# Attention of a two-layer decoder: the negative maximum and the first exponential of a row of scores are issued ahead of the filling work, evacuations queue behind them in one tile, and the reciprocals are turned one block later

## The chip, the cores and the metric

The kernel runs on one core of a Trainium2 chip. A core has a matrix engine (TensorE, PE in the profile), a vector engine (VectorE, DVE), an activation engine (ScalarE, ACT), GpSimd (POOL) and a queue engine (SyncE, SP). Each engine works through its own list of instructions in the order in which they stand in the program, and waits on semaphores for the others. The metric is the device time of one execution in microseconds (us).

## The reference

A model of two layers on 2048 tokens of width 1024: a Mamba-2 mixer, then causal attention with 16 heads over keys and values made once from a compressed latent, then an output projection and a last norm, all in float32. The part that the change touches is the attention:

```python
s = einsum('bqhd,bkhd->bhqk', q_nope, k_nope) + einsum('bqhr,bkr->bhqk', q_rope, k_rope)
s = s.astype(float32) * scale
p = softmax(where(mask, s, -inf), axis=-1)
o = einsum('bhqk,bkhd->bqhd', p, v)
```

## The kernel before

The program has three stages after each other: the Mamba layer with all projections, the attention (`heads`, from L1181), and the output projection (`back`). In the attention, the work on PE is issued in the order in which the Python code records it (a manual schedule for PE alone). For DVE, ACT, POOL and SP a list scheduler puts the recorded instructions in an order at build time; on the chip that order is fixed, and an instruction that waits holds back all that stand behind it on its engine.

Each of the 16 heads has four blocks of 512 queries (qb 0 to 3). A block has four query tiles of 128 queries (j 0 to 3). The scores of a query tile against all keys up to the diagonal are computed in banks of up to 512 keys: one bank for qb 0, two for qb 1, three for qb 2, four for qb 3. Below, **S qb.j.n** is the n-th bank of scores of query tile j. The steps for a query tile, in `scores` (L1197):

- S: three matmuls (L88 to L90, fp16 in high and low halves) into a PSUM bank with the tag `mm`; there are four such banks. In the last bank a fourth matmul adds the causal mask (L1220).
- DVE takes the maximum of each bank (`mx`, L1221) and, after the last one, the negative maximum over all of them (`nm`, L1225).
- ACT takes exp(s + nm) of each bank into `Pr` (L1233) and sums the row beside it. Only then is the `mm` bank free for a later S. In the profile this exponential is an ACTIVATE followed by a short ACTIVATION_READ_ACCUMULATOR, which carries the release. These are put on a list `late` and recorded one by one before the score banks of the next query tile.
- DVE adds the sums of the banks to one number per row (`sum`, L1237).

The exponentials become an output in two more steps, for each block of queries and each of its 4qb+4 tiles of 128 keys (kb):

- **T qb.kb** (`turn`, L1243): up to four transposes on PE (L1248) into a bank with the tag `tr`, of which there are four too; ACT evacuates the high half (`PTs`, L119), DVE the low half (L120).
- **V qb.kb** (`values`, L1254): two matmuls (L1258, L1259) that add the product with the values to the output bank of the block, also a `tr` bank. After the last kb, ACT copies that bank out (`Os`, L1265), and two DMAs add its halves in memory.

What fills PE while a query tile's maximum and exponentials run is the T and V work of a block that lies up to 20 banks of scores back. The table CREDIT (L44) says, for each qb, j and bank, which T and V units are recorded after that bank. After the last block of a head, DVE takes the reciprocals of the 16 sums per row (`ri`, L1274 and L1275), PE turns them (L1277) into a `tr` bank, ACT copies them (`rT`, L1279), and they go to memory.

Of the kernel before, what the change touches and what calls it, by code (L numbers as in the profile page):

```python
# [21 lines left out]
P = 128  # L22
# [22 lines left out]
    (("VT",), ("TV",), ("VT",), ("TV",)),  # L45
    (("", "VTVT"), ("", "TTVV"), ("", "TTVV"), ("", "TTVV")),
    (("TT", "", "VVTV"), ("TV", "", "VTTV"), ("TV", "", "TTVV"), ("TTV", "", "TVV")),
    (("T", "", "", "VVTTVTV"), ("T", "V", "", "VTTVTV"), ("T", "V", "V", "TVTTV"), ("TV", "V", "", "TVTVT")),
)
MAGIC = 12582912.0  # L50
PSCALE = 32768.0
# [20 lines left out]
class Net:  # L72
# [1108 lines left out]
    def heads(self, sp):  # L1181
# [15 lines left out]
        def scores(h, qb, st):  # L1197

            if h + 1 < NH:
                if qb == 2:  # L1200
                    self.load_k(h + 1, 0, NB)
                    self.load_v(h + 1)
                self.load_q(h + 1, qb)
            Q, K = quer.pop((h, qb)), keys[h]
            late = []
            for j in range(4):
                qs = slice(j * P, (j + 1) * P)
                parts = cuts(qb * TB + (j + 1) * P)
                nb = len(parts)
                mx = self.t(sp, "mx", [P, 4], bufs=4)  # L1210
                banks = []
                for n, (c0, w) in enumerate(parts):
                    if late:
                        late.pop(0)()
                    begun.append(0)
                    s = self.t(self.pp, "tr" if len(begun) <= 18 and len(begun) % 2 == 1 else "mm", [P, TB], bufs=4)
                    ks = slice(c0, c0 + w)
                    self.mm3(s[:, :w], Q[:, 0, qs], Q[:, 1, qs], K[:, 0, ks], K[:, 1, ks], True, n < nb - 1)
                    if n == nb - 1:
                        nc.tensor.matmul(s[:, w - P:w], self.idb, self.mk, start=False, stop=True)  # L1220
                    v.tensor_reduce(mx[:, n:n + 1], s[:, :w], AX.X, ALU.max)  # L1221
                    banks.append((s, w))
                    yield CREDIT[qb][j][n]
                nm = self.t(sp, "nm", [P, 1], bufs=4)
                v.tensor_reduce(nm, mx[:, :nb], AX.X, ALU.max, negate=True)  # L1225
                p = {}
                sm = self.t(sp, "sm", [P, 4], bufs=4)
                st["P"].append(p)

                def exp(n, j=j, nb=nb, parts=parts, banks=banks, nm=nm, p=p, sm=sm):  # L1230
                    s, w = banks[n]
                    x = self.t(sp, "Pr", [P, TB], bufs=NP)
                    nc.scalar.activation(x[:, :w], s[:, :w], AF.Exp, bias=nm, accum_out=sm[:, n:n + 1])  # L1233
                    for c in range(0, w, P):
                        p[(parts[n][0] + c) // P] = x[:, c:c + P]
                    if n == nb - 1:
                        v.tensor_reduce(sums[h][:, 4 * qb + j:4 * qb + j + 1], sm[:, :nb], AX.X, ALU.add)  # L1237

                late += [lambda n=n, f=exp: f(n) for n in range(nb)]
            for f in late:  # L1240
                f()

        def turn(h, qb, kb, st):  # L1243

            jj = max(kb - 4 * qb, 0)
            pt = self.t(self.pp, "tr", [P, TB], bufs=4)
            for j in range(jj, 4):
                nc.tensor.transpose(pt[:, j * P:(j + 1) * P], st["P"][j][kb], self.ident)  # L1248
# [14 lines left out]
        def finish(h, qb, st):  # L1263
# [8 lines left out]
            if qb == NB - 1:  # L1272
                ri = self.t(sp, "ri", [P, 16], bufs=2)
                v.reciprocal(ri, sums[h])  # L1274
                v.tensor_scalar(ri, ri, 0.5, None, ALU.mult)  # L1275
                ps = self.t(self.pp, "tr", [P, TB], bufs=4)
                nc.tensor.transpose(ps[:16, 0:P], ri, self.ident)  # L1277
# [7 lines left out]
        def ahead():  # L1285
            for n, (h, qb) in enumerate(jobs):
                if qb == 0:
                    sums[h] = self.t(sp, "sum", [P, 16], bufs=3)
                yield from scores(h, qb, states[n])

        units = [(h, qb, kb, states[n]) for n, (h, qb) in enumerate(jobs) for kb in range(4 * qb + 4)]
# [11 lines left out]
        step = 0  # L1303
# [206 lines left out]
```

## Time and profile before

| what | value |
|---|---|
| time, median of 3 runs | 3100.96 us (3096.12 to 3102.59) |
| time of the profiled execution | 3099.32 us |
| its span, first to last instruction | 3097.2 us, so 2.1 us lie around it |
| busy in the span | PE 97%, DVE 75%, ACT 63%, POOL 20% |
| attention, from the first bank of scores to the last transposes | 2007.8 to 2906.5 us |
| one head of the attention in the middle | 55.63 us |

A row of the timeline gives the start in us from the start of the span, the length, the engine, the line, the operation, output and inputs by the program's tile names, how many instructions are merged in it, and, in brackets, how long the engine sat idle just before and what ended that. A matmul row is longer than the time until the next matmul can start: matmuls are pipelined, and rows of 0.38 us start every 0.22 us. So a wait of PE is the distance between two starts less 0.22 us (for 512 columns; 0.16 for 384, 0.11 for 256, 0.06 for 128), which is up to 0.16 us more than the idle time in brackets.

### The profile page before, as it was taken

To read this page: it belongs to the slowest core of one execution; us is meant where nothing else is said; L and a number is where in the kernel's file an instruction comes from. 1 tells how busy PE (TensorE), PEld (TensorE's weight loads), DVE (VectorE), ACT (ScalarE), POOL (GpSimd) and SP (SyncE) were. 2 spreads that over 40 slices of the span, in tenths; PEclk is the share of its full clock that TensorE was granted. 3 is DMA by queue.
4 is the path that set the end of the run, shared out by engine and by line. 5 is a ranking of instruction groups with operands and counts; after the bars stand their busy time and mean duration, and the time that the engine had idled before them with its cause. 6 is when DMAs were issued, how large, how long until landed. Compare 5 with 4: busy or idle time off the path is not lost.

```text
span 3097.2 us, 51355 instructions
## 1 busy us (share of the span) xinstructions
PE 2994.5 (97%) x17758; PEld 1759.2 (57%) x17758; DVE 2330.1 (75%) x5306; ACT 1936.4 (63%) x4920; POOL 615.3 (20%) x842
## 2 busy tenths in 40 slices
PE   7899999999999999999999999999999999999998
PEld 3466655555455554545555555456666666665777
DVE  7789887777777687797755453488888888888576
ACT  8777566665667656565534333388888888888422
POOL 0211122211222112222111212322122222222100
PEclk9999999999999999999999999999999999999999
DMA  8675436445454466364466555622223222232485
GB/s 298 221 235 181 151 106 220 129 158 163 153 191 162 131 207 222 121 199 145 145 214 197 194 173 170 197 49 60 55 56 67 54 58 57 54 88 75 130 261 158
DMA packets 205065, 457.11 MB, mean 148 GB/s; under 512 B 28114, under 2 KB 57554, under 8 KB 203364
## 3 DMA queue, kind: packets, MB, share of 16 engines
q1 hardware_dynamic: 176948, 375.94, 37.9%
q0 software_dynamic: 27856, 77.89, 9.8%
q8 instruction: 140, 2.29, 0.3%
q14 instruction: 121, 0.99, 0.1%
HBM read 340.99 MB, written 112.73 MB: 146 GB/s over the span
## 4 chain that ended last, share of the span: by engine, by line
PE 40%; DVE 5%; ACT 4%; issue 3%; DMA 2%; POOL 0%; SPq 0%; ACTq 0%; POOLq 0%; DVEq 0%
PE mm L88 7%; PE mm L90 6%; PE mm L89 6%; PE tr L1248 6%; PE tr L1259 3%; PE tr L1258 3%; PE tr L88 3%; PE tr L90 3%; PE tr L89 3%; ACT Pr L1233 2%; DVE PTs L120 1%; DMA os<-ri_d 1%; ACT PTs L119 1%; DVE mx L1221 1%; PE mm L1220 0%
## 5 line engine op out<-in xcount | busy, mean ns | idle before, releaser
L120 DVE SCALAR_TENSOR_TENSOR PTs<-tr,PTs 128x512 f16<-128x512 f32 (+3 forms) x640 | 374.2, 606 | 76.8 <-ACT PTs L119 69.7
L1233 ACT ACTIVATE Pr<-mm,nm 128x512 f32<-128x512 f32 (+2 forms) x631 | 394.2, 635 | 49.4 <-DVE nm L1225 44.9
L1221 DVE TENSOR_REDUCE mx<-mm 128x1 f32<-128x512 f32 (+2 forms) x631 | 373.1, 604 | 31.1 <-PE mm L90 28.3
L119 ACT ACTIVATE PTs<-tr 128x512 f16<-128x512 f32 (+3 forms) x640 | 329.4, 544 | 97.9 <-PE tr L1248 95.9
L1248 PE MATMUL tr<-pack,Pr 128*128 128x128 f32 x2176 | 317.5, 273 | 1.8 <-ACT Os L1265 1.4
L88 PE MATMUL mm<-xT,wsp 128*128 128x512 f16 x800 | 305.7, 382 | 7.9 <-ACT wsp L119 4.9
L89 PE MATMUL mm<-xT,wsp 128*128 128x512 f16 x800 | 304.6, 381 | 0.0
L90 PE MATMUL mm<-xT,wsp 128*128 128x512 f16 x800 | 303.6, 380 | 0.0
L1248 PEld LDWEIGHTS tr<-pack,Pr 128*128 128x128 f32 x2176 | 253.2, 141 | 68.9 <-ACT Os L1265 2.2
L88 PE MATMUL mm<-K,xT 96*128 96x512 f16 (+2 forms) x639 | 222.4, 348 | 27.5 <-ACT Pr L1233 24.0
L88 PE MATMUL mm<-wsp,xT 128*128 128x512 f16 (+1 forms) x640 | 232.0, 363 | 4.3 <-ACT craw L610 4.1
L89 PE MATMUL mm<-wsp,xT 128*128 128x512 f16 (+1 forms) x640 | 232.3, 363 | 3.0 <-DVE wsp L120 3.0
L89 PEld LDWEIGHTS <-xT 128*128 128x128 f16 (+1 forms) x1408 | 138.0, 98 | 168.1 <-issue 69.6
L616 DVE SCALAR_TENSOR_TENSOR cacc<-craw,pack,cacc 128x512 f32<-128x512 f32 x288 | 219.3, 790 | 18.0 <-ACT cacc L614 17.2
L90 PE MATMUL mm<-wsp,xT 128*128 128x512 f16 (+1 forms) x640 | 232.5, 364 | 0.0
L90 PE MATMUL mm<-K,xT 96*128 96x512 f16 (+2 forms) x639 | 221.8, 347 | 0.0
L89 PE MATMUL mm<-K,xT 96*128 96x512 f16 (+2 forms) x639 | 221.2, 346 | 0.0
L1258 PE MATMUL tr<-PTs,xT 128*128 128x512 f16 (+3 forms) x640 | 221.0, 347 | 0.1
L1259 PE MATMUL tr<-PTs,xT 128*128 128x512 f16 (+3 forms) x640 | 219.1, 347 | 0.0
L90 PEld LDWEIGHTS <-xT 128*128 128x128 f16 (+1 forms) x1408 | 136.9, 97 | 133.1 <-issue 5.7
L88 PEld LDWEIGHTS <-xT 128*128 128x128 f16 (+1 forms) x1408 | 137.7, 98 | 120.1 <-issue 8.5
L88 PE MATMUL mm<-wsp,yT 128*128 128x512 f16 (+1 forms) x512 | 197.4, 385 | 0.9 <-DVE sz L640 0.5
(456 smaller groups left out, 6795.8 us busy)
## 6 DMA issues: line engine op xcount, KB each, us to landing
wsp<-wi_d SPq DMA_DIRECT2D x96, 512.0 KB, 3.6
big<-cumT SPq DMA_DIRECT2D x64, 512.0 KB, 4.8
wraw<-in_ssm_w_out_dram SPq DMA_DIRECT2D x96, 256.0 KB, 3.6
wi_d<-wsp SPq DMA_DIRECT2D x32, 512.0 KB, 3.8
wsp<-wo_d SPq DMA_DIRECT2D x32, 512.0 KB, 3.5
wsp<-wu_d SPq DMA_DIRECT2D x28, 512.0 KB, 3.8
hx<-in_ssm_w_in_dram SPq DMA_DIRECT2D x48, 256.0 KB, 4.8
wraw<-in_ssm_w_in_dram SPq DMA_DIRECT2D x48, 256.0 KB, 4.4
```

The source lines that it names most:

```text
L88: mm(out, l_hi, r_hi, start=start, stop=False)
L89: mm(out, l_hi, r_lo, start=False, stop=False)
L90: mm(out, l_lo, r_hi, start=False, stop=stop)
L119: self.nc.scalar.activation(hi, src, AF.Copy, scale=scale)
L120: self.nc.vector.scalar_tensor_tensor(lo, src, scale, hi, ALU.mult, ALU.subtract)
L616: nc.vector.scalar_tensor_tensor(acc, raw[:, k:k + TB], wk[k], acc, ALU.mult, ALU.add)
L1221: v.tensor_reduce(mx[:, n:n + 1], s[:, :w], AX.X, ALU.max)
L1233: nc.scalar.activation(x[:, :w], s[:, :w], AF.Exp, bias=nm, accum_out=sm[:, n:n + 1])
L1248: nc.tensor.transpose(pt[:, j * P:(j + 1) * P], st["P"][j][kb], self.ident)
L1258: nc.tensor.matmul(st["O"][:, c], vals[h][:, kb, :], u[:, 0], start=kb == 0, stop=False)
L1259: nc.tensor.matmul(st["O"][:, c], vals[h][:, kb, :], u[:, 1], start=False, stop=kb == nk - 1)
```

## The change

Five things, all in the attention:

1. The negative maximum `nm` is recorded directly after the last maximum of a query tile, before the T and V units that CREDIT puts behind that bank; it used to be recorded after them. With one bank (qb 0) the maximum itself is taken with a minus sign, and `nm` falls away.
2. Where a query tile has three or four banks (qb 2 and 3), its first exponential is recorded directly after `nm` too.
3. In the first query tile of qb 3 (j 0, four banks) a list `pins` makes the evacuations of the T units that follow it stand behind that `nm` on DVE and behind that first exponential on ACT.
4. The sums of a block's four query tiles go to one tile, and DVE adds them up in one instruction per block (none for qb 0, where ACT writes the sum itself), not one per query tile.
5. The reciprocals are computed where they were, but turned by PE and copied by ACT after the output of the next head's first block, and CREDIT is changed for the first two query tiles of qb 3: the T unit after the first bank of j 0 goes to the end of j 0, and one T and one V unit from the end of j 0 go to the first bank of j 1.

```diff
-    (("T", "", "", "VVTTVTV"), ("T", "V", "", "VTTVTV"), ("T", "V", "V", "TVTTV"), ("TV", "V", "", "TVTVT")),
+    (("", "", "", "TVVTTV"), ("TVT", "V", "", "VTTVTV"), ("T", "V", "V", "TVTTV"), ("TV", "V", "", "TVTVT")),
...
-            late = []
+            late, total = [], sums[h][:, 4 * qb:4 * qb + 4]
+            sm = self.t(sp, "sm", [P, 4, 4], bufs=2) if qb else total.unsqueeze(2)
...
-                    v.tensor_reduce(mx[:, n:n + 1], s[:, :w], AX.X, ALU.max)
                     banks.append((s, w))
+                    if nb == 1:
+                        v.tensor_reduce(nm, s[:, :w], AX.X, ALU.max, negate=True)
+                    else:
+                        v.tensor_reduce(mx[:, n:n + 1], s[:, :w], AX.X, ALU.max)
+                    if n == nb - 1:
+                        if nb > 1:
+                            self.last_max = v.tensor_reduce(nm, mx[:, :nb], AX.X, ALU.max, negate=True)
+
+                        def exp(n, j=j, nb=nb, parts=parts, banks=banks, nm=nm, p=p):
+                            s, w = banks[n]
+                            x = self.t(sp, "Pr", [P, TB], bufs=NP)
+                            self.last_exp = nc.scalar.activation(x[:, :w], s[:, :w], AF.Exp, bias=nm,
+                                                                 accum_out=sm[:, j, n:n + 1])
+                            for c in range(0, w, P):
+                                p[(parts[n][0] + c) // P] = x[:, c:c + P]
+                            if j == 3 and n == nb - 1 and nb > 1:
+                                v.tensor_reduce(total, sm[:, :, :nb], AX.X, ALU.add)
+
+                        late += [lambda n=n, f=exp: f(n) for n in range(nb)]
+                        if nb > 2:
+                            late.pop(0)()
+                        if nb > 3 and j == 0:
+                            pins[:] = [self.last_max, self.last_exp]
                     yield CREDIT[qb][j][n]
-                nm = self.t(sp, "nm", [P, 1], bufs=4)
-                v.tensor_reduce(nm, mx[:, :nb], AX.X, ALU.max, negate=True)
...
-            self.pair16(u[:, 0, c], u[:, 1, c], pt[:, c], PSCALE)
+            with ExitStack() as order:
+                for pin in pins:
+                    order.enter_context(self.tc.issue_after(pin.ins))
+                self.pair16(u[:, 0, c], u[:, 1, c], pt[:, c], PSCALE)
...
                 v.tensor_scalar(ri, ri, 0.5, None, ALU.mult)
+                inverse.append((h, ri))
+            if inverse and (qb == 0 or h == NH - 1):
+                h, ri = inverse.pop()
                 ps = self.t(self.pp, "tr", [P, TB], bufs=4)
                 nc.tensor.transpose(ps[:16, 0:P], ri, self.ident)
...
         for credit in ahead():
             step += 1
             if step > LAG:
                 for what in credit:
                     work(what)
+            pins.clear()
```

The diff tells what is recorded; where the scheduler then puts it is another matter. Three places, all in the eighth head (heads 2 to 14 have the same order).

**First place: DVE, end of qb 2.** Before, from the last two maxima of S 2.3 on (`mx_5665`, from the banks `mm_5677` and `mm_5679`): the sum of the tile before, the negative maximum (`nm_5683`), the low half of T 1.0 (`PTs_5681`), then the first maxima of qb 3.

```order
L1221 TENSOR_REDUCE mx_5665_27502<-mm_5677_27537 128x1
L1221 TENSOR_REDUCE mx_5665_27502<-mm_5679_27545 128x1
L1237 TENSOR_REDUCE sum_5543_27076<-sm_5664_27501 128x1
L1225 TENSOR_REDUCE nm_5683_27564<-mx_5665_27502 128x1
L120 SCALAR_TENSOR_TENSOR PTs_5681_27556<-tr_5680_27551,PTs_5681_27556 128x512
L1221 TENSOR_REDUCE mx_5689_27578<-mm_5690_27579 128x1
```

After the change, the same stretch (`mx_5566` is the maxima, `nm_5567` the negative maximum, `PTs_5581` the low half of T 1.0, `nm_5588` the negative maximum of S 3.0, `PTs_5595` that of T 1.1):

```order
L1228 TENSOR_REDUCE mx_5566_27272<-mm_5577_27303 128x1
L1228 TENSOR_REDUCE mx_5566_27272<-mm_5578_27308 128x1
L120 SCALAR_TENSOR_TENSOR PTs_5581_27322<-tr_5580_27317,PTs_5581_27322 128x512
L1231 TENSOR_REDUCE nm_5567_27273<-mx_5566_27272 128x1
L1228 TENSOR_REDUCE mx_5587_27340<-mm_5589_27342 128x1
L1228 TENSOR_REDUCE mx_5587_27340<-mm_5590_27347 128x1
L1241 TENSOR_REDUCE sum_5452_26866<-sm_5525_27117 128x4
L1228 TENSOR_REDUCE mx_5587_27340<-mm_5591_27352 128x1
L1228 TENSOR_REDUCE mx_5587_27340<-mm_5592_27357 128x1
L1231 TENSOR_REDUCE nm_5588_27341<-mx_5587_27340 128x1
L120 SCALAR_TENSOR_TENSOR PTs_5595_27371<-tr_5594_27366,PTs_5595_27371 128x512
```

Here the negative maximum of S 2.3 has moved behind the low half of T 1.0, while that of S 3.0 stands directly behind its maxima, ahead of T 1.1.

**Second place: ACT, start of qb 3.** Before, from the last exponential of S 2.3 (`Pr_5687`): T 1.1, the copy of the output of qb 0 (`Os_5696`), T 1.2 to T 1.4, then the four exponentials of S 3.0 (their first is `Pr_5707`).

```order
L1233 ACTIVATE Pr_5687_27571,sm_5684_27566<-mm_5679_27545,nm_5683_27564 128x512
L119 ACTIVATE PTs_5692_27589<-tr_5691_27584 128x512
L1265 ACTIVATE Os_5696_27612<-tr_5682_27559 128x512
L119 ACTIVATE PTs_5698_27621<-tr_5697_27616 128x512
L119 ACTIVATE PTs_5700_27629<-tr_5699_27624 128x512
L119 ACTIVATE PTs_5703_27640<-tr_5702_27635 128x512
L1233 ACTIVATE Pr_5707_27649,sm_5705_27647<-mm_5690_27579,nm_5704_27645 128x512
L1233 ACTIVATE Pr_5711_27663,sm_5705_27647<-mm_5693_27592,nm_5704_27645 128x512
```

After the change (`Pr_5584` is the last exponential of S 2.3, `Pr_5593` and `Pr_5606` the first two of S 3.0, `PTs_5595` T 1.1, `PTs_5600` T 1.2, `rT_5598` the copy of the turned reciprocals of the head before):

```order
L1236 ACTIVATE Pr_5584_27332,sm_5525_27117<-mm_5578_27308,nm_5567_27273 128x512
L1236 ACTIVATE Pr_5593_27364,sm_5586_27339<-mm_5589_27342,nm_5588_27341 128x512
L119 ACTIVATE PTs_5595_27371<-tr_5594_27366 128x512
L1277 ACTIVATE Os_5596_27378<-tr_5582_27325 128x512
L1294 ACTIVATE rT_5598_27384<-tr_5597_27382 16x128
L119 ACTIVATE PTs_5600_27392<-tr_5599_27387 128x512
L1236 ACTIVATE Pr_5606_27408,sm_5586_27339<-mm_5590_27347,nm_5588_27341 128x512
```

The first exponential of S 3.0 has moved ahead of T 1.1 and of the copy of qb 0's output; the other three now alternate with evacuations. On PE, T 1.3 now takes the `tr` bank that this copy frees (before, T 1.4 did), and V 1.0 opens its output bank in the one that the copy `rT` frees.

**Third place: DVE, qb 0 of the next head.** Before, from the negative maximum of S 0.1 on (`nm_5556`): the last sum of the head before, the reciprocal, the low half of T 2.9 of the head before (`PTs_5548`), a sum, the maximum of S 0.2 (`mx_5558`).

```order
L1225 TENSOR_REDUCE nm_5556_27118<-mx_5551_27100 128x1
L1237 TENSOR_REDUCE sum_5317_26274<-sm_5538_27066 128x1
L1274 RECIPROCAL ri_5673_27527<-sum_5317_26274 128x16
L120 SCALAR_TENSOR_TENSOR PTs_5548_27094<-tr_5547_27090,PTs_5548_27094 128x384
L1237 TENSOR_REDUCE sum_5543_27076<-sm_5550_27099 128x1
L1221 TENSOR_REDUCE mx_5558_27121<-mm_5560_27125 128x1
```

After the change (`nm_5460` and `nm_5466` are the negative maxima of S 0.1 and S 0.2, now taken at once; `PTs_5458` is the low half of T 2.9):

```order
L1226 TENSOR_REDUCE nm_5460_26889<-mm_5462_26892 128x1
L1241 TENSOR_REDUCE sum_5239_26094<-sm_5373_26567 128x4
L1286 RECIPROCAL ri_5575_27298<-sum_5239_26094 128x16
L1226 TENSOR_REDUCE nm_5466_26907<-mm_5468_26910 128x1
L120 SCALAR_TENSOR_TENSOR PTs_5458_26885<-tr_5457_26881,PTs_5458_26885 128x384
```

The maximum of S 0.2 has moved ahead of the low half of T 2.9.

More of the change, by code (lines that the diff above doesn't have):

```diff
@@ L1209, in scores @@
                 nb = len(parts)
-                mx = self.t(sp, "mx", [P, 4], bufs=4)
+                mx, nm = (self.t(sp, m, [P, n], bufs=4) for m, n in (("mx", 4), ("nm", 1)))
+                p = {}
+                st["P"].append(p)
                 banks = []
@@ L1220, in scores @@
                         nc.tensor.matmul(s[:, w - P:w], self.idb, self.mk, start=False, stop=True)
-                    v.tensor_reduce(mx[:, n:n + 1], s[:, :w], AX.X, ALU.max)
                     banks.append((s, w))
-                    yield CREDIT[qb][j][n]
-                nm = self.t(sp, "nm", [P, 1], bufs=4)
[L1225 to L1237, printed above, removed]
@@ L1239, in scores @@
-                late += [lambda n=n, f=exp: f(n) for n in range(nb)]
+                    if nb == 1:
[19 more added lines that the diff above has]
+                            pins[:] = [self.last_max, self.last_exp]
@@ L1289, in ahead @@
                 yield from scores(h, qb, states[n])
+        inverse = []
         units = [(h, qb, kb, states[n]) for n, (h, qb) in enumerate(jobs) for kb in range(4 * qb + 4)]
@@ L1301, in work @@
                 values(*a, u, c)
-        step = 0
+        step, pins = 0, []
         for credit in ahead():
```

## The prediction

> **What bounds the kernel now.** I read the summary first, then the attention in windows of one head, then PE's waits there, then the timeline around each of them.
>
> ```profile
> PE 2994.5 (97%) x17758; PEld 1759.2 (57%) x17758; DVE 2330.1 (75%) x5306; ACT 1936.4 (63%) x4920; POOL 615.3 (20%) x842
> ...
> 2328.96:2384.60 55.64, 54.18 (x356) 35.35 (x354) 47.50 (x114) 45.31 (x126) 12.15 (x20) 1.00 0.28 57
> 2384.60:2440.23 55.63, 54.17 (x356) 35.35 (x353) 47.56 (x114) 45.30 (x126) 12.14 (x20) 1.00 0.28 59
> ...
> PE mm L88 <- ACT Pr L1233: 24.0, 26, 1.9
> ```
>
> The two rows of windows are two heads of the attention: length, then busy time of PE, weight loads, DVE, ACT and POOL, then the granted clock (1.00). The heads repeat to 0.01 us, so one head stands for all but the first and the last. PE sets the period; DVE is busy 47.5 of 55.6 us, ACT 45.3. The last row is PE's only large wait in the attention: score matmuls waiting for an exponential to free a bank. Most of it is one place per head, the opening of the second query tile of qb 3 (S 3.1.0):
>
> ```profile
> 2420.93 1.29 DVE L120 SCALAR_TENSOR_TENSOR PTs<-tr,PTs 128x512 f16<-128x512 f32 x2
> 2422.14 0.15 DVE L1225 TENSOR_REDUCE nm<-mx 128x1 f32<-128x4 f32 x1
> 2422.32 0.69 ACT L1233 ACTIVATE Pr<-mm,nm 128x512 f32<-128x512 f32 x1
> 2423.00 0.68 ACT L1233 ACTIVATE Pr<-mm,nm 128x512 f32<-128x512 f32 x1
> 2421.56 0.38 PE L1259 MATMUL tr<-PTs,xT 128*128 128x512 f16 x1
> 2423.15 0.38 PE L88 MATMUL mm<-K,xT 96*128 96x512 f16 x1 [1.21 <-ACT Pr L1233]
> ```
>
> PE could go on at 2421.56 + 0.22 = 2421.78 and starts at 2423.15: **1.37 us** per head. The negative maximum stands behind two low halves (1.29 us) on DVE. After an exponential starts, its bank is free 0.83 us later (2422.32 to 2423.15), and the next one on ACT starts 0.68 us later.
>
> **The change part by part, per head.**
>
> *Removed: the wait at S 3.1.0, -1.37.* With negative maximum and exponential ahead of the evacuations, the bank is free long before PE gets there.
>
> *Added at S 3.0.1.* In the first place of the order rows, the negative maximum of S 2.3 now stands behind the low half of T 1.0. The rows of today:
>
> ```profile
> 2416.07 0.60 ACT L119 ACTIVATE PTs<-tr 128x512 f16<-128x512 f32 x1
> 2416.53 0.16 DVE L1225 TENSOR_REDUCE nm<-mx 128x1 f32<-128x3 f32 x1
> 2416.56 0.38 PE L88 MATMUL mm<-K,xT 96*128 96x512 f16 x1
> 2416.70 0.69 DVE L120 SCALAR_TENSOR_TENSOR PTs<-tr,PTs 128x512 f16<-128x512 f32 x1
> 2416.72 0.69 ACT L1233 ACTIVATE Pr<-mm,nm 128x512 f32<-128x512 f32 x1
> 2417.21 0.60 PE L1248 MATMUL tr<-pack,Pr 128*128 128x128 f32 x4
> 2417.65 0.38 PE L88 MATMUL mm<-K,xT 96*128 96x512 f16 x1
> ```
>
> S 3.0.0 starts at 2416.56, T 1.1 at 2417.21, S 3.0.1 at 2417.65, without a wait. The low half cannot start before its high half ends (2416.67), so it stays at 2416.70. The negative maximum follows it by 0.60 (two low halves in 1.29 us, the second starting 0.60 after the first), at 2417.30 in place of 2416.53; the exponential 0.19 later, as now, at 2417.49; its bank, which S 3.0.1 needs, is free at 2417.49 + 0.83 = 2418.32. T 1.1 no longer stands between, so PE is ready at 2417.21: **+1.11 us**. Behind the waiting negative maximum on DVE stand the first maxima of qb 3; they wait for PE anyway. The next two exponentials follow at 0.68 us and PE's banks at 0.65, so S 3.0.2 and S 3.0.3 lose up to 0.1 more; I take +0.08. If DVE were early enough, the wait would still be 2416.72 + 0.83 - 2417.21 = 0.34, since T 1.1 is gone: bounds 0.34 and 1.2.
>
> *Added at T 1.3.* In the second place of the order rows, the copy of qb 0's output waits behind the first exponential of S 3.0 and T 1.1, and T 1.3 needs the bank it frees. From the start of S 3.0.3, with the durations of these rows:
>
> ```profile
> 2386.68 0.41 DVE L1221 TENSOR_REDUCE mx<-mm 128x1 f32<-128x256 f32 x1
> 2418.89 0.27 PE L88 MATMUL mm<-K,xT 96*128 96x256 f16 x1
> 2419.21 0.22 PE L1220 MATMUL mm<-mk,idb 128*128 128x128 bf16 x1
> 2419.27 0.27 PE L1258 MATMUL tr<-PTs,xT 128*128 128x256 f16 x1
> 2419.60 0.50 PE L1248 MATMUL tr<-pack,Pr 128*128 128x128 f32 x3
> 2419.80 0.60 ACT L1265 ACTIVATE Os<-tr 128x512 f32<-128x512 f32 x1 [0.47 <-PE tr L1259]
> 2420.30 1.08 ACT L119 ACTIVATE PTs<-tr 128x512 f16<-128x512 f32 x2
> ```
>
> Matmuls and mask end after 0.54 (2419.21 + 0.22 - 2418.89); maximum 0.41, which makes 0.95, with 0.03 for the hand-over 0.98; the negative maximum starts then, the exponential 0.19 later, at 1.17; T 1.1's high half 0.68 later, at 1.85; the copy 0.50 later (2419.80 to 2420.30 is the distance of two copies on ACT), at 2.35; it lasts 0.60 and the bank is free at about 3.0. PE has until then S 3.0.3 (0.38), T 1.1 and T 1.2 (0.44 each, 2417.21 to 2417.65), V 0.2 and V 0.3 (0.33, 2419.27 to 2419.60) and the turned reciprocals (a quarter of a T unit, 0.11), together 1.70: **+1.30 us**. What is queued behind the copy on ACT is `rT` and T 1.2; V 1.0 waits for `rT`, but 0.44 after T 1.3 begins, which hides its 0.25 us. The other three exponentials of S 3.0 now alternate with evacuations: the second starts about 1.2 us after the copy, so S 3.1.1 has its bank at about 2.35 + 1.2 + 0.83 = 4.4, and PE arrives after T 1.3, V 1.0, S 3.1.0, T 1.4, V 1.1 and T 1.5, at about 5.7. Hidden.
>
> *Added at T 3.0, and removed waits.* Third place, and the small waits of today:
>
> ```profile
> 2387.24 0.22 PE L1220 MATMUL mm<-mk,idb 128*128 128x128 bf16 x1
> 2387.60 0.25 DVE L1274 RECIPROCAL ri<-sum 128x16 f32<-128x16 f32 x1
> 2387.79 0.56 DVE L120 SCALAR_TENSOR_TENSOR PTs<-tr,PTs 128x384 f16<-128x384 f32 x1
> 2388.32 0.55 DVE L1221 TENSOR_REDUCE mx<-mm 128x1 f32<-128x384 f32 x1
> 2388.54 0.39 PE L1248 MATMUL tr<-pack,Pr 128*128 128x128 f32 x2
> ...
> 2401.51 0.14 DVE L1225 TENSOR_REDUCE nm<-mx 128x1 f32<-128x2 f32 x1
> 2401.69 0.69 ACT L1233 ACTIVATE Pr<-mm,nm 128x512 f32<-128x512 f32 x1 [1.18 <-DVE nm L1225]
> 2402.07 0.32 PE L90 MATMUL mm<-K,xT 96*128 96x384 f16 x1
> 2402.52 0.27 PE L88 MATMUL mm<-K,xT 96*128 96x256 f16 x1
> ...
> 2405.93 0.38 PE L1259 MATMUL tr<-PTs,xT 128*128 128x512 f16 x1
> 2406.37 0.38 PE L88 MATMUL mm<-K,xT 96*128 96x512 f16 x1
> 2409.79 0.38 PE L1259 MATMUL tr<-PTs,xT 128*128 128x512 f16 x1
> 2410.14 0.38 PE L88 MATMUL mm<-K,xT 96*128 96x512 f16 x1
> 2413.70 0.22 PE L1259 MATMUL tr<-PTs,xT 128*128 128x128 f16 x1
> 2413.89 0.28 PE L1277 MATMUL tr<-pack,ri 128*16 128x128 f32 x1
> ```
>
> T 3.0 (2388.54) needs the bank that the low half of T 2.9 frees (2387.79 + 0.56 = 2388.35). Now the maximum of S 0.2 (0.55, its scores ready at 2387.46) goes first, after the reciprocal, so that low half starts 0.5 later and ends at about 2388.82: **+0.33**. Removed: the negative maximum at 2401.51 stood behind two low halves and goes ahead of them, which ends the wait at 2402.52 (0.29) and, through an earlier exponential, those at 2406.37 (0.22) and 2410.14 (0.13); the turn of the reciprocals waited 0.13 at 2413.89 and needs nothing in its new place. **-0.77** in all. Against that, in qb 2 and at the end of qb 3 an evacuation moves behind an exponential that used to follow it (T 3.14, T 0.1, T 2.5): PE had no slack at S 2.2.2, and a 256-wide copy costs ACT some 0.35: +0.30, and -0.08 at S 3.3.2.
>
> *Sums and small maxima removed.* DVE loses 208 of 256 `sum` and 64 of 256 `nm`, each 0.15 us: 41 us of DVE, 2.5 per head. I cost it at nothing beyond the waits above, because DVE idles 8 of 55.6 us and the waits named end at an instruction of ACT or at a low half that waits for ACT. The Trainium skill, "VectorE: DVE Perf Modes", Rules for kernel authors, says to minimise the count of chained VectorE instructions, since each pays its own flush. By that rule alone the change gains, up to 2.5 us per head; by the rows it gains what the rival below works out.
>
> *DMAs.* None is added; the store of the reciprocals goes out a block later and is first read after the attention. The last head turns its reciprocals where it did.
>
> Sum per head: -1.37 + 1.11 + 0.08 + 1.30 + 0.33 - 0.77 + 0.30 - 0.08 = **+0.90 us**. Heads 2 to 15 have this order: 14 x 0.90 = 12.6. The first head has no head before it to turn or to wait for and the last none after it; I take nothing for both (bounds -2 and +2). The profiled execution took 3099.3 us (span 3097.2), which becomes 3111.9; the median of the runs is 1.6 higher, which gives **3113.5**, slower by 0.4%.
>
> **Rivals.** (a) *The stall closes and nothing takes its place*: DVE runs so far ahead without its sums that the low half of T 1.0 costs nothing and the output copy goes through early. Then -1.37 - 0.77 - 0.08 + 0.33 + 0.30 = -1.6 per head, 3079. It decides if S 3.0.1 finds its bank without a wait. For it: the negative maxima of S 1.3 and S 3.0 do move ahead. Against it: a fixed order on ACT, in which the copy cannot start before an exponential that needs S 3.0.3. (b) *Even*: the wait at S 3.0.1 stays at its lower bound of 0.34 and T 3.0 is covered: 0.90 - 0.77 - 0.33 = -0.2 per head, 3098; with half of these costs 3106. For it: DVE gets 2.5 us. (c) *More new waits*: with ACT's evacuations between the exponentials, S 3.1.2, S 3.1.3 or the banks of T 1.4 to T 1.7 run late too; one more evacuation of 0.60 in the way makes +1.5 per head, 3122. (d) *Fewer DVE instructions*: if each of some eight waits of a head that pass through DVE shrank by one 0.15 us instruction, -1.2 per head, 3084. Against: PE's named waits follow full-size instructions, not sums. That the change does not do what it says is (a)'s opposite and is in the forecast: at S 2.3 the scheduler puts the negative maximum behind the filling work.
>
> **How the numbers follow.** Forecast 0.52 (own range 3107 to 3119), (c) 0.20, (b) 0.18, (a) 0.07, (d) 0.03. About 0.2% (6.2 us) is what a measurement of this kernel can tell from no change: faster means under 3094.8, slower over 3107.2. Slower: 0.52 + 0.20 = 0.72; same: 0.18; faster: 0.10. The range runs from (b) to a little above (c): 3096 to 3123.
>
> **What the profile would show.** A head of 56.5 us in place of 55.63. No wait at S 3.1.0; a wait of about 1.1 us at S 3.0.1 on an exponential; one of about 1.3 at T 1.3 on the output copy; about 0.3 at T 3.0 on a low half; none at S 2.0.2. The prediction is wrong if S 3.0.1 or T 1.3 does not wait, or if heads differ among themselves.

## The result: 0.4% slower, and the profile after

The changed kernel takes 3112.28 us (median of 6 runs, 3108.97 to 3113.41), the kernel before 3099.30 us in the same job (6 runs, 3093.22 to 3103.76): a ratio of 1.0038 with a 95% interval of 1.0027 to 1.0048. The profiled execution took 3113.41 us, its span is 3111.4, 14.2 more than before.

The summary of the changed kernel, busy time by engine:

```profile
PE 2994.7 (96%) x17758; PEld 1761.2 (57%) x17758; DVE 2312.6 (74%) x5034; ACT 1931.6 (62%) x4920; POOL 616.7 (20%) x842
```

The windows of two heads, columns as in the prediction:

```profile
2332.03:2388.38 56.35, 53.91 (x356) 35.30 (x354) 46.53 (x97) 45.02 (x127) 12.15 (x20) 1.00 0.28 57
2388.38:2444.73 56.35, 53.91 (x356) 35.29 (x354) 46.40 (x97) 45.02 (x127) 12.15 (x20) 1.00 0.28 57
```

A head takes **56.35 us in place of 55.63**, with 97 instructions on DVE in place of 114 and no more busy time on any engine. The loss is waiting. PE's waits in the attention, grouped (line, what it waited for, us in total, times, longest):

```profile
PE tr L1257 <- ACT Os L1277: 21.0, 15, 3.7
PE mm L88 <- ACT Pr L1236: 19.4, 23, 1.1
PE tr L1257 <- DVE PTs L120: 3.0, 16, 0.4
```

Before, the second row stood at 24.0, and the first at 1.4, a single wait in the 15th head. The timeline shows both, here in one head from the end of qb 2 to S 3.1.0:

```profile
2419.78 0.68 DVE L120 SCALAR_TENSOR_TENSOR PTs<-tr,PTs 128x512 f16<-128x512 f32 x1
2420.01 0.38 PE L90 MATMUL mm<-K,xT 96*128 96x512 f16 x1
2420.38 0.15 DVE L1231 TENSOR_REDUCE nm<-mx 128x1 f32<-128x3 f32 x1
2420.56 0.69 ACT L1236 ACTIVATE Pr<-mm,nm 128x512 f32<-128x512 f32 x1 [0.88 <-DVE nm L1231]
2421.39 0.38 PE L88 MATMUL mm<-K,xT 96*128 96x512 f16 x1 [1.00 <-ACT Pr L1236]
...
2423.83 0.16 DVE L1231 TENSOR_REDUCE nm<-mx 128x1 f32<-128x4 f32 x1
2423.99 0.60 PE L1257 MATMUL tr<-pack,Pr 128*128 128x128 f32 x4
2424.02 0.69 ACT L1236 ACTIVATE Pr<-mm,nm 128x512 f32<-128x512 f32 x1 [1.34 <-DVE nm L1231]
2424.70 0.59 ACT L119 ACTIVATE PTs<-tr 128x512 f16<-128x512 f32 x1
2425.18 0.60 ACT L1277 ACTIVATE Os<-tr 128x512 f32<-128x512 f32 x1
2425.83 0.66 PE L1257 MATMUL tr<-pack,Pr 128*128 128x128 f32 x4 [1.24 <-ACT Os L1277]
...
2426.54 0.38 PE L1271 MATMUL tr<-PTs,xT 128*128 128x512 f16 x1
2426.75 0.38 PE L88 MATMUL mm<-K,xT 96*128 96x512 f16 x1
```

The first five rows are S 3.0.1. PE is ready at 2420.01 + 0.22 = 2420.23 and starts at 2421.39: **1.16 us**. The low half of T 1.0 holds the negative maximum back, that the exponential, and that the bank; how much of the wait this makes up, e1 below tells. The group behind is T 1.3: T 1.2 starts at 2423.99 and takes 0.44, so PE is ready at 2424.43 and starts at 2425.83: **1.40 us**. It needs the bank of the output copy, which stands on ACT behind the first exponential and the evacuation of T 1.1. In the last two rows S 3.1.0 follows its predecessor by 0.21: the old wait of 1.37 is gone. The third place, T 3.0 in qb 0 of the next head:

```profile
2391.34 0.49 DVE L1226 TENSOR_REDUCE nm<-mm 128x1 f32<-128x384 f32 x1
2391.75 1.14 DVE L120 SCALAR_TENSOR_TENSOR PTs<-tr,PTs 128x384 f16<-128x384 f32 x3
2392.04 0.22 PE L1223 MATMUL mm<-mk,idb 128*128 128x128 bf16 x1
2392.43 0.63 PE L1257 MATMUL tr<-pack,Pr 128*128 128x128 f32 x4 [0.17 <-DVE PTs L120]
```

The maximum of S 0.2 precedes the low half, and T 3.0 starts 0.39 after the mask, 0.33 more than the mask's pitch of 0.06.

**Where the 14.2 us lie**, by the starts of the heads: first head -0.70; heads 2 to 14 +9.62 (13 x 0.72, and 0.28 once); the 15th head **+4.10** (61.72 against 57.62 us); the last head and all behind it +1.23. The 15th head was not foreseen. The timeline of the changed kernel there, and its windows of 4 us:

```profile
2819.76 0.60 PE L1257 MATMUL tr<-pack,Pr 128*128 128x128 f32 x4
2820.03 1.06 ACT L1348 ACTIVATE W<-wr 128x1024 fp32r<-128x1024 f32 x1 [1.58 <-DMA wr<-in_mla_w_out_dram]
2821.29 1.06 ACT L1348 ACTIVATE W<-wr 128x1024 fp32r<-128x1024 f32 x1 [0.21 <-DMA wr<-in_mla_w_out_dram]
2822.26 0.67 ACT L1236 ACTIVATE Pr<-mm,nm 128x512 f32<-128x512 f32 x1
2823.40 0.59 ACT L1277 ACTIVATE Os<-tr 128x512 f32<-128x512 f32 x1
2824.04 0.86 PE L1257 MATMUL tr<-pack,Pr 128*128 128x128 f32 x4 [3.68 <-ACT Os L1277]
```

```profile
2820.00:2824.00 4.00, 0.36 (x4) 0.12 (x2) 0.46 (x1) 3.77 (x7) 2.83 (x2) 1.00 0.56 171
2824.00:2828.00 4.00, 3.96 (x15) 2.39 (x16) 1.84 (x4) 2.31 (x8) 1.82 (x1) 0.57 0.71 180
```

In this head the weights of the output projection are loaded, and ACT converts them (`W`, L1348). Two conversions, the first waiting 1.58 us for its transfer, stand ahead of the first exponential of S 3.0, and the output copy stands behind that. T 1.3 waits 3.84 us (2819.76 + 0.44 to 2824.04), and then the granted clock falls to 0.57 for 4 us. In the kernel before only one conversion stood at this place, 1.54 us late, and PE waited 1.55 us:

```profile
2810.38 1.06 ACT L1331 ACTIVATE W<-wr 128x1024 fp32r<-128x1024 f32 x1 [1.54 <-DMA wr<-in_mla_w_out_dram]
```

### The profile page after: what moved, and what is told of

It is laid out like the page before. It is cut to its first block, busy times and chain, and to the rows that moved or that the text cites. A ratio compares the mean times of both kernels' runs of the same rounds, so it can differ in the third digit from the quotient of the medians.

```text
span 3111.4 us, 51032 instructions
## 1 busy us (share of the span) xinstructions
PE 2994.7 (96%) x17758; PEld 1761.2 (57%) x17758; DVE 2312.6 (74%) x5034; ACT 1931.6 (62%) x4920; POOL 616.7 (20%) x842
## 4 chain that ended last, share of the span: by engine, by line
PE 37%; DVE 6%; ACT 5%; issue 3%; DMA 3%; SPq 0%; POOL 0%; ACTq 0%; DVEq 0%; POOLq 0%
PE tr L1257 6%; PE mm L88 6%; PE mm L90 5%; PE mm L89 5%; PE tr L1270 3%; PE tr L1271 3%; PE tr L88 2%; PE tr L90 2%; PE tr L89 2%; ACT Pr L1236 2%; ACT PTs L119 1%; DVE PTs L120 1%; DMA os<-ri_d 1%; DVE mx L1228 1%; DMA o_d<-Os 0%
## 5 line engine op out<-in xcount | busy, mean ns | idle before, releaser
L1228 DVE TENSOR_REDUCE mx<-mm 128x1 f32<-128x512 f32 (+2 forms) x569 | 336.3, 617 | 36.9 <-PE mm L90 34.2
```

## The experiments

All are edits of the changed kernel, but for e7, which is one of the kernel before. What precedes the attention moved by up to 8.7 us between profiled executions (the first bank of scores starts at 2004.35 in one, at 2013.09 in another), so I compare heads, which repeat to 0.02 us within a kernel, and not single spans. (In the changed kernel and its edits one or two heads, the tenth among them, take 0.28 longer; the cause of that stays open.) A head in the table is the mean of heads 4 to 8. The ratio is to the kernel before in the same job, whose median lay between 3098.28 and 3101.53.

| kernel | head, us | 15th head | time, us | ratio to before, 95% |
|---|---|---|---|---|
| before | 55.63 | 57.62 | 3099.30 | 1 |
| the change | 56.35 | 61.72 | 3112.28 | 1.0038 (1.0027 to 1.0048) |
| e1, pin in qb 2 | 55.87 | 60.31 | 3104.24 | 1.0009 (0.9999 to 1.0018) |
| e2, no pins | 55.69 | 58.42 | 3100.72, one run | |
| e3, credits as before | 55.36 | 58.41 | 3093.10 | 0.9988 (0.9979 to 0.9998) |
| e4, other credits | 55.60 | 60.57 | 3101.53 | 1.0004 (0.9994 to 1.0013) |
| e5, e4 and e1 | 55.13 | 60.95 | 3092.88 | 0.9976 (0.9967 to 0.9985) |
| e6, reciprocals in the old place | 55.55 | 58.45 | 3097.44, one run | |
| e7, before with the sums alone | 55.18 | 58.24 | 3089.65 | 0.9976 (0.9967 to 0.9985) |
| e8, weights a head earlier | 56.36 | 56.58 | 3116.67 | 1.0054 (1.0036 to 1.0071) |
| e10, low half first | 55.97 | 58.84 | 3099.56, one run | |
| e13, e3 and e1 | 54.89 | 58.33 | 3087.11 | 0.9966 (0.9953 to 0.9979) |
| e15, late conversions | 56.35 | 56.55 | 3108.73 | 1.0035 (1.0023 to 1.0048) |
| e16, e13, e10 and e15 | 54.53 | 54.69 | 3082.86 | 0.9950 (0.9936 to 0.9964) |

**e1: the negative maximum of S 2.3 ahead of the low half of T 1.0.**

```diff
                         if nb > 3 and j == 0:
                             pins[:] = [self.last_max, self.last_exp]
+                        elif qb == 2 and j == 3:
+                            pins[:] = [self.last_max]
```

> The changed kernel with one more pin: the low half of T 1.0 also queues behind the negative maximum of S 2.3 on VectorE, as in the kernel before. Nothing else moves. Theory A (the two new waits behind fixed queues are the loss): the wait at S 3.0.1 falls from 1.16 to about 0.55 us, the one at T 1.3 stays at 1.40, a head goes from 56.35 to 55.75 us, the time to about 3104. Rival B (the loss comes from the order on the matrix engine, four banks of scores without filling work between them, whatever stands ahead of the negative maximum): the head stays at 56.35 and the time at 3112.

The head falls by 0.48 to 55.87. S 3.0.1 waits 0.70 in place of 1.16, T 1.3 waits its 1.40 as in the change. So the low half ahead of the negative maximum costs 0.47. The rest of the wait can be read from the traces of the eighth head. 0.34 of it is the lower bound of the prediction, left uncovered since T 1.1 is gone from this place. The other 0.35 comes from DVE: the last maximum of S 2.3 starts 0.39 us ahead of S 3.0.0, where it started 0.75 ahead of it in the kernel before. On ACT the first exponential of S 2.2 now stands ahead of the high half of T 0.1, and DVE sits idle until that half has come, here in the changed kernel:

```profile
2416.99 0.56 DVE L120 SCALAR_TENSOR_TENSOR PTs<-tr,PTs 128x384 f16<-128x384 f32 x1 [0.36 <-ACT PTs L119]
```

PE, too, reaches S 2.3.1 0.25 earlier, without the turn of the reciprocals (0.11) and its wait (0.14). No run takes this part away by itself.

**e4 and e5: the credits between old and new; and the same with e1's pin.** The T unit stands behind the first bank of j 0 again, the pair at the first bank of j 1 stays where the change has it.

```diff
-    (("", "", "", "TVVTTV"), ("TVT", "V", "", "VTTVTV"), ...
+    (("T", "", "", "VVTTV"), ("TVT", "V", "", "VTTVTV"), ...
```

> The changed kernel with T 1.1 back between S 3.0.0 and S 3.0.1; the negative maximum of S 2.3 still stands behind the low half of T 1.0, and on ScalarE the output copy now stands ahead of the first exponential of S 3.0. Theory A: the wait at S 3.0.1 falls by the 0.44 us of T 1.1 to 0.72, the one at T 1.3 vanishes, S 3.1.0 waits about 0.5 again; a head takes 55.0 us, the time is about 3093. Rival B: only the 0.44 us come back, 55.9 us a head, 3106.

> Both edits of the two runs before together. Theory A: the wait at S 3.0.1 falls to 0.1 or less, none at T 1.3, about 0.5 at S 3.1.0; a head takes 54.4 us, the time is about 3086, faster than both kernels. Rival B: as the run with T 1.1 moved back, 3106.

The gain came out at 0.75 us per head in place of 1.35 (e4) and 1.22 in place of 1.95 (e5). The wait at T 1.3 shrank to 0.22, and S 3.1.0 waits 0.34 where about 0.5 was expected (0.30 and 0.23 in e5). A wait at S 3.2.0 grew from 0.17 to 0.73, which nobody had priced. Its bank is freed by the first exponential of S 3.1. The last maxima of S 3.1 stand on DVE behind the low halves of T 1.4 and T 1.5, as in the change, and the negative maximum now stands behind that of T 1.6 as well: it starts 0.90 after the last maximum in place of 0.45. S 3.0.1 still waits 0.73 in e4; with the pin 0.26.

**e3 and e13: the credits as before; and with e1's pin.**

```diff
-    (("", "", "", "TVVTTV"), ("TVT", "V", "", "VTTVTV"), ...
+    (("T", "", "", "VVTTVTV"), ("T", "V", "", "VTTVTV"), ...
```

> The change with its table of credits as it was before (T 1.1 back between S 3.0.0 and S 3.0.1, T 1.3 back ahead of S 3.1.0), all else as in the change. The theory of the prediction, that the moved place of T 1.3 (copy of the output, 1.40 us of wait per head) and of T 1.1 (S 3.0.1 left without cover, 1.16) is what the gain of S 3.1.0 is paid with: both waits go, head of 55.0 us against 56.35, about 3093 us. If the order on ScalarE and VectorE (the pinned maximum, the reciprocals) makes the loss and not the table: the head stays at 56.2 or more, 3110.

> The kernel of e3 (credits as before) with one more pin: in query block 2 the filling work behind tile 3 waits for its last maximum too. If e1's gain of 0.48 us per head came from S 3.0.1's lead alone, which the old credits already give, nothing is added: head of 55.0, as e3. If the pin brings the low halves behind the maxima as well, another 0.3: 54.7, about 3089 us.

With the old table the head is 55.36, 0.99 under the change: T 1.3 waits 0.22 and S 3.0.1 0.72. It is 0.36 more than expected, since T 1.1, back between S 3.0.0 and S 3.0.1, covers only its 0.44 of the 1.16, and since S 3.1.1 now waits 0.53 for the second exponential, which stands on ACT behind three evacuations. e13 adds the pin and gains another 0.47, as e1 did. Its rival, that the old credits already give this lead, falls.

**e10: on DVE, the maximum of S 0.2 behind the low half of T 2.9.**

```diff
                     if nb == 1:
-                        v.tensor_reduce(nm, s[:, :w], AX.X, ALU.max, negate=True)
+                        with ExitStack() as order:
+                            if j == 2 and h:
+                                order.enter_context(self.tc.issue_after(self.lows[-2].ins))
+                            v.tensor_reduce(nm, s[:, :w], AX.X, ALU.max, negate=True)
```

(`self.lows` keeps the last low halves.)

> The change with one order more: on VectorE the maximum of S 0.2 is issued behind the low half of T 2.9. The prediction's term: T 3.0 waits 0.33 because that low half stands behind the maximum. Then the wait goes and the head falls from 56.35 to 56.0, the span by 5 us. If T 3.0 was released by something else, or the exponential of S 0.2 now holds a bank: head of 56.35 or more.

The wait at T 3.0 is gone and the head is 55.97, as expected.

**e6: the reciprocals turned in the old place.**

```diff
-                inverse.append((h, ri))
-            if inverse and (qb == 0 or h == NH - 1):
-                h, ri = inverse.pop()
```

> The change with one part undone: the reciprocals are turned in the old place, behind query block 3, and not a block later. The order then puts the negative maximum of S 2.3 ahead of the low half of T 1.0, and no rT stands behind the output's copy. Theory (lead of S 3.0.1 set by that low half, as in e1): S 3.0.1 waits 0.7 instead of 1.16, T 1.3 still waits 1.4 for the copy; with the turned reciprocals' old wait of 0.14 the head is 55.9 to 56.0. If rT was what T 1.3 waited for: T 1.3's wait falls under 1.1 and the head to 55.6.

PE's waits of this kernel, grouped:

```profile
PE tr L1270 <- ACT Os L1277: 15.1, 15, 2.5
PE tr L1289 <- DVE PTs L120: 6.1, 14, 0.5
PE mm L88 <- ACT Pr L1236: 4.7, 10, 1.1
```

My expectation missed. The head falls by 0.80, to 55.55, and T 1.3 does not wait for the copy at all. Without the turn between V 0.3 and T 1.2, the banks go to other tiles: V 1.0 opens its output in the bank of the copy, a T unit (0.44) later in PE's list, and waits 1.06 (1.40 + 0.11 for the turn that is gone, less 0.44, is 1.07). The turn itself waits 0.59 for a bank (0.14 before), ahead of S 2.3.1. That delays PE, the negative maximum of S 2.3 stands ahead of the low half of T 1.0 again, and S 3.0.1 then waits only 0.17. So about half of the 0.80 lies at the turn and S 3.0.1 (0.59 + 0.17 in place of 1.16) and nearly all of the rest at the copy (1.06 in place of 1.40). The move of the turn did take the turn's own wait out of qb 2, but S 3.0.1 waits longer for it, and the copy's bank went to the T unit that needs it first.

**e2: no pins.**

```diff
-                        if nb > 3 and j == 0:
-                            pins[:] = [self.last_max, self.last_exp]
```

> The change without its pins: the filling work's evacuations are not issued behind the negative maximum and the first exponential. ScalarE then evacuates T 1.1 ahead of the exponential of S 3.0.0, VectorE's order stays. Theory, that the table of credits and not the pins sets the waits: T 1.3 still waits about 1.4 for the copy, S 3.0.1 waits 1.2 to 1.7 since its bank comes free an evacuation (0.59) later; head of 56.2 to 56.9. If the pins make the loss: the head falls under 55.8.

The same place as in the second group above, now without pins (T 1.1 on ACT, T 1.2 on PE, negative maximum, exponential, low half of T 1.1, copy, T 1.3):

```profile
2419.89 0.60 ACT L119 ACTIVATE PTs<-tr 128x512 f16<-128x512 f32 x1 [1.14 <-PE tr L1255]
2419.91 0.16 DVE L1231 TENSOR_REDUCE nm<-mx 128x1 f32<-128x4 f32 x1
2420.07 0.60 PE L1255 MATMUL tr<-pack,Pr 128*128 128x128 f32 x4
2420.39 0.68 ACT L1236 ACTIVATE Pr<-mm,nm 128x512 f32<-128x512 f32 x1
2420.52 0.69 DVE L120 SCALAR_TENSOR_TENSOR PTs<-tr,PTs 128x512 f16<-128x512 f32 x1 [0.46 <-ACT PTs L119]
2421.05 0.60 ACT L1275 ACTIVATE Os<-tr 128x512 f32<-128x512 f32 x1
2421.27 0.66 PE L1255 MATMUL tr<-pack,Pr 128*128 128x128 f32 x4 [0.60 <-DVE PTs L120]
```

Here too I was wrong: the head is 55.69. ACT evacuates T 1.1 in the 1.14 us in which it sat idle anyway, the exponential starts 0.29 later against the negative maximum than with the pin (0.48 in place of 0.19 after it starts), and T 1.3 takes the bank of T 1.1 and waits for its low half, 0.76 in place of 1.40. S 3.0.1 is unchanged at 1.16. The pin put the exponential, which nobody needed so soon, ahead of an evacuation that PE did need.

**e7: the sums alone, on the kernel before.** The sums of a block in one instruction, the negative maximum of qb 0 taken at once; nothing else.

```diff
+                    if nb == 1:
+                        v.tensor_reduce(nm, s[:, :w], AX.X, ALU.max, negate=True)
...
-                    if n == nb - 1:
-                        v.tensor_reduce(sums[h][:, 4 * qb + j:4 * qb + j + 1], sm[:, :nb], AX.X, ALU.add)
+                    if j == 3 and n == nb - 1 and nb > 1:
+                        v.tensor_reduce(total, sm[:, :, :nb], AX.X, ALU.add)
```

> The kernel before with one part of the change alone: the sums of a query block are added in one instruction, and the negative maximum of block 0 is taken at once, which takes some 14 short VectorE instructions from a head; no order is changed otherwise. My theory, that VectorE's time lies beside TensorE's except where a bank waits for it: 55.4 to 55.6 us a head against 55.63, 3096 to 3101 us. The rival of fewer VectorE instructions: 54.4 us, 3084.

The window of one head of it:

```profile
2378.91:2434.10 55.19, 53.75 (x355) 35.35 (x353) 46.34 (x97) 45.11 (x126) 12.12 (x20) 1.00 0.27 58
```

55.18 us, a gain of 0.45 and of 0.24% in time: more than I expected, less than the rival's 1.2. Waits tell why. Those at S 2.0.2, S 2.1.1, S 2.2.1, S 3.3.1 and S 3.3.2 (0.81 together) are gone, the one at T 3.0 (0.34) is new, the one at S 3.1.0 still is 1.37. In the eighth head the scheduler now puts the negative maximum of S 1.3 ahead of two low halves although it is recorded in its old place.

**e8 and e15: the conversions of the weights.** e8 loads them one head earlier, e15 leaves the loads and issues the conversions on ACT behind an exponential of the last head.

```diff
-            if h == NH - 3:
+            if h == NH - 4:
```

> The changed kernel with the loads of the output projection's weights one head earlier. In the changed kernel the 15th head alone takes 61.7 us: its T 1.3 waits 3.85 us behind two conversions of weights on ScalarE, the first of which waits for its load, and then the granted clock falls to 0.57 for 4 us. Theory A (the load is late): the wait there falls to 1.4 to 2 us, the clock stays at 1.00, the 15th head takes 58 us or less, the time is about 3108.5. Rival (the conversions themselves, 1.06 us each, hold the queue whenever their weights come): at least 2.1 us more than in other heads remain, 3111 or more.

```diff
+                            if h == NH - 1 and qb == 1 and j == 0:
+                                self.mark = self.last_exp
...
-                nc.scalar.activation(hi, self.wraw[k], AF.Copy)
+                with self.tc.issue_after(self.mark.ins):
+                    nc.scalar.activation(hi, self.wraw[k], AF.Copy)
```

> The change with one order more: the conversions of the output projection's weights are issued behind the first exponential of query block 1 in the last head, so that none stands in the 15th head. Theory, that two conversions waiting for their transfers ahead of S 3.0's exponential cost the 15th head 4.1 us: that head falls from 61.1 to 56.4 like the others, the clock stays over 0.95 there, and the time falls by 3 to 4 us, to about 3109 us, if the conversions cost nothing where they land. If the last head then waits for them or the output projection starts late: 3113 or more. If the 15th head stays at 60 us or more without them, the conversions were not its cause.

In e8 the wait only moves to the 14th head, which takes 61.80 us; the scheduler puts the conversions right behind their loads, wherever these are. The rows of e8's timeline:

```profile
2768.16 1.06 ACT L1348 ACTIVATE W<-wr 128x1024 fp32r<-128x1024 f32 x1 [1.88 <-DMA wr<-in_mla_w_out_dram]
2769.56 1.06 ACT L1348 ACTIVATE W<-wr 128x1024 fp32r<-128x1024 f32 x1 [0.35 <-DMA wr<-in_mla_w_out_dram]
...
2772.31 0.66 PE L1257 MATMUL tr<-pack,Pr 128*128 128x128 f32 x4 [4.12 <-ACT Os L1277]
```

In e15 the 15th head is like the others but for 0.2 us, and its clock is whole:

```profile
2782.91:2839.47 56.56, 54.01 (x356) 35.30 (x353) 46.51 (x97) 45.13 (x126) 8.71 (x13) 1.00 0.34 82
```

So the conversions' place on ACT is the cause, and an earlier load does not help, since they follow it. The 15th head gains 5.17 us: 2.44 of wait at T 1.3 (3.84 less 1.40), 1.7 by the clock (4 us at 0.57), and about 1 in other waits (0.53 at S 2.1.1 and 0.35 at a T unit of that head, 0.2 at the first bank of the next), which are gone too. The time gains less surely: 10.45 us over before, against 12.98 for the change, with overlapping intervals.

**e16: all repairs.** e13, with e10's order and e15's.

> All repairs together, on the change: credits as before (e3), the pin in query block 2 (e13), the low half of T 2.9 issued ahead of the maximum of S 0.2, and the late weight conversions (e15). By e13's head of 54.89 less the wait of T 3.0 (0.34): 54.55, that is 4.8 us on 14 heads under e13, and 3 to 4 us in the 15th head by e15: about 3079 us, faster than before by 0.6%. If the low half's move only shifts the maximum of S 0.2 and with it a wait to S 0.3: head of 54.9, 3083. If the conversions cost the last head in this order what they save the 15th: 3083 to 3087.

The windows of one head and of the 15th:

```profile
2375.72:2430.26 54.54, 53.88 (x356) 35.26 (x353) 46.20 (x97) 44.93 (x126) 12.13 (x20) 1.00 0.28 59
2758.04:2812.72 54.68, 53.95 (x355) 35.27 (x353) 46.22 (x97) 45.03 (x126) 8.71 (x13) 1.00 0.35 85
```

54.53 us a head, and 3082.86 us in all (3078.13 to 3084.97): faster than both kernels, than the one before by 0.5%. Heads and 15th head came out as expected. The missing 4 us are where the third case put them: what follows the start of the last head takes 266.7 us against 263.7 in e13, so in this order the late conversions cost the last head and what follows it 3.0 of what they save, by one trace of each.

## Why the prediction was right, point by point

The forecast, 3113.5 us, is 1.2 off and its sign holds; of the rivals, (a), (b) and (d) did not happen in the changed kernel, and (c) did not in its ordinary heads. It is not as good as it looks: two misses cancel, and the wait at S 3.0.1 has its size in part from a cause that the prediction did not name.

| step of the prediction | predicted, us per head | measured |
|---|---|---|
| wait at S 3.1.0 removed | -1.37 | -1.37 |
| S 3.0.1 | +1.11 | +1.16 |
| S 3.0.2, S 3.0.3 | +0.08 | +0.08 |
| T 1.3, output copy | +1.30 | +1.40 |
| T 3.0, low half behind the maximum of S 0.2 | +0.33 | +0.34 |
| small waits removed (S 2.0.2, S 2.1.1, S 2.2.1, turn) | -0.77 | -0.79 |
| S 2.2.2 | **+0.30** | **0** |
| S 3.3.2 | -0.08 | -0.08 |
| the rest (S 3.2.0, S 3.3.1 and what no row names) | 0 | -0.02 |
| head | +0.90 | +0.72 |
| 15th head | +0.90 | **+4.10** |
| first head; last head and all behind it | 0 (-2 to +2) | -0.70; +1.23 |

- **The waits** at S 3.0.1, T 1.3 and T 3.0 stand where they were put and within 0.1 us. They are the same in every ordinary head. e1 and e10 take two of the causes away. The low half of T 2.9 was worth all of its 0.33, but that of T 1.0 only 0.47 of the 0.77 worked out (1.11 less the lower bound of 0.34). The prediction left the maxima of S 2.3 where they stood, and they come 0.35 later; that this filled the gap is luck. With T 1.1 back between the banks and the pin on (e13), S 3.0.1 still waits 0.26, where the prediction's working leaves nothing (0.34 less 0.44).
- **The mis-sized term is S 2.2.2.** It was priced against PE's slack of the kernel before, as if an evacuation of 0.35 us had been put between two exponentials and nothing else had moved. But the negative maximum ahead of them starts 0.44 earlier relative to S 2.1.2 (1.66 us behind it in place of 2.10, in the eighth head), which covers the evacuation. This gain was already in the sum, as the end of the wait at S 2.2.1, and the step did not carry it on to the next bank.
- **The step that was missing** is the 15th head. "Heads 2 to 15 have this order" holds for what PE does, not for ACT, where the conversions stand in the 15th alone; the prediction read a middle head of the trace and not that one. The row of the kernel before, with its conversion 1.54 us late ahead of the output copy, was there to be seen. 13 x 0.18 too much (2.3) and 3.2 too little made the total right.
- **Sums and small maxima** were costed at nothing beyond the waits named. e7 shows where those removed waits come from: the sums, with the single maximum of qb 0, end 0.81 of small waits and bring the 0.34 at T 3.0, while the other negative maxima are recorded where they were. So -0.77 and +0.33 were the right sizes, but of the first 0.64 was put down to the wrong part of the change: the negative maximum of S 1.3 goes ahead of the low halves in e7 too, where it is recorded in its old place. (The turn's 0.13 is not among the waits that e7 ends.) DVE's busy time fell by 17.5 us for 272 instructions, 0.064 each, and not by the 0.15 of their rows: rows on DVE overlap (a negative maximum starts at 2420.38, the next maximum at 2420.44). By the Trainium skill, "VectorE: DVE Perf Modes", Rules for kernel authors, fewer chained VectorE instructions gain. e7 agrees in sign, with 0.45 us per head.
- **What the change is paid with.** The sums take 0.45 off a head (e7), and with the other parts it comes from 55.18 to 56.35. Undone alone, in the changed kernel, the credits are worth 0.99, the turn of the reciprocals 0.80, the pins 0.66. These do not add up, since all three act on the same chain, from the negative maximum of S 3.0 over its exponential and T 1.1 to the copy of the output. The negative maximum and first exponential ahead of the filling work, without any of these three, were not tried by themselves.

## What to carry to other kernels

An instruction moved ahead in a fixed order pays only if something waits for it: here an exponential whose bank PE takes 2.73 us after its start (2424.02 to 2426.75, of which 1.40 are the new wait), where 0.83 would do, went ahead of an evacuation and a copy whose banks PE needed at once. When a wait is taken out, list what stands behind the moved instruction on its engine and which bank each of these frees, and look at the heads in which other work runs too, not at a middle one alone. A sum should carry an earlier start on to the banks behind it, and not price each against the old slack.

## What the runs showed of the hardware that was not expected

The granted clock fell after waits of PE in some runs and not in others of about the same length. In e1 a wait was enough that shows 2.77 us idle:

```profile
2816.15 0.66 PE L1259 MATMUL tr<-pack,Pr 128*128 128x128 f32 x4 [2.77 <-ACT Os L1279]
```

In e10 one of 3.34 was not, and the clock stayed at 1.00 behind it:

```profile
2814.49 0.65 PE L1260 MATMUL tr<-pack,Pr 128*128 128x128 f32 x4 [3.34 <-ACT Os L1280]
```

In e4 two short ones within 3 us sufficed:

```profile
2810.02 0.38 PE L1270 MATMUL tr<-PTs,xT 128*128 128x512 f16 x1 [1.19 <-ACT Os L1277]
...
2811.78 0.38 PE L88 MATMUL mm<-K,xT 96*128 96x512 f16 x1 [1.16 <-ACT Pr L1236]
```

What tells them apart is where the waits lie. In each of the fourteen traces the granted clock changes only at times that are whole multiples of 3.413 us apart, and each fall in the attention lasted one such stretch, at 0.50 (in the change from 2824.36 to 2827.77). Below are stretches of this grid around the waits of e1, e4 and e10; the second number is PE's busy time, the third from the end the clock. In e1, the stretch with the wait and the next:

```profile
2813.40:2816.81 3.41, 0.66 (x5) 0.58 (x6) 0.76 (x2) 3.41 (x8) 2.27 (x1) 1.00 0.65 201
2816.81:2820.23 3.42, 3.42 (x11) 1.86 (x10) 1.91 (x3) 2.06 (x6) 0.07 (x1) 0.50 0.62 163
```

In e4, the stretch ahead of the fall:

```profile
2808.82:2812.23 3.41, 1.06 (x6) 0.40 (x5) 0.00 (x0) 3.41 (x8) 2.66 (x2) 1.00 0.68 187
```

In e10, the two stretches over which the wait is spread:

```profile
2809.46:2812.87 3.41, 1.68 (x17) 1.39 (x15) 1.04 (x5) 2.19 (x3) 1.26 (x1) 1.00 0.97 317
2812.87:2816.28 3.41, 1.79 (x11) 1.23 (x12) 1.40 (x3) 3.41 (x10) 3.40 (x2) 1.00 0.38 112
```

PE is idle for 2.75 us of its stretch in e1 and for 2.35 in e4. In e10 an edge of the grid cuts the wait in two, and PE is idle for 1.73 and 1.62 us. The other falls in the attention came after stretches with 3.09 us idle (the change), 2.71 (e5), 2.49 (e8, whose wait of 4.12 us is cut in two as well) and 1.85 (e7). Over the whole of these programs but their first 130 us, a fall followed every stretch at full clock with more than 1.98 us idle and none with less than 1.73; in between both occur. In the change the price was 1.7 us, in its 15th head.

The Trainium skill, "TensorE: Matmul & The Clock Gate", Part 1, says that the clock halves after at least one idle window of some 3.4 us, and that these windows run on their own, without regard to when work starts. The traces agree with the second, and with the length of the window. They differ on the first: in no fall of the attention did PE idle through a whole window, and in e7 1.85 us of one were enough; there the measurement decides. How idle time is counted, between 1.73 and 1.98 us, stays open.
